# Sparse attention's sliding branch: values and weights in two fp32r parts in place of a native fp32 product, and one ring of rows with one buffer

## The chip, the core and the metric

The program runs on one core of a Trainium2 chip. The metric is the device time of one execution in microseconds (us). A core has TensorE (PE: matrix products; PEld is its loading of stationary operands), VectorE (DVE), ScalarE (ACT), GpSimd (POOL) and SyncE (SP, which here only issues DMAs). Each engine works through its own instructions in a fixed order and waits at an instruction until what it needs has been signalled.

## The reference, cut to what matters

Two blocks of a first kind (stick-breaking and windowed attention, gated, with an MLP) are followed by one block of a second kind: a state-space mixer and a sparse attention, gated and summed, and then a mixture of 32 experts. Sequence 512, width 1024, float32. The change is in the sparse attention. It has 16 heads in two groups of 8, head size 64, and three branches for each head, whose outputs are weighed by gates g:

```
s = q @ k.T * 64 ** -0.5                      # for each branch its own keys
p = softmax(s where the branch's mask allows)
out = g0 * p_cmp @ v_cmp + g1 * p_sel @ v_sel + g2 * p_win @ v_win
```

The compressed branch sees 31 block summaries, the selected branch 4 blocks of 64 tokens, the window branch (window 512, which is the whole sequence, so it is a causal softmax) every earlier token. The change concerns the product `p_win @ v_win` alone.

## The kernel before

Nearly every product is made from operands in two parts: a high part `hi` of type fp32r and the rest `lo = x - hi`, also fp32r, so that `x @ w` is `hi @ w_hi + hi @ w_lo + lo @ w_hi`. `K.split` (line 193 for the subtraction on DVE, line 187 for the high part on POOL) makes the parts. Weights come in 532 tiles of 128x1024: SP loads a raw tile `w_st` (three buffers), POOL writes `w_hi`, DVE writes `w_lo`.

The sparse attention (`Block2.nsa`) walks over 2 groups x 4 token blocks (`tb`), each in 2 halves of four heads, and in each half first the selected branch (`br` 0), then the window branch (`br` 1). `nsa_branch` makes the weights: for each head two products into `ps_b`, a masked minimum on DVE (line 1498, `mx`), an exponential on ACT (line 203, with the sum `sm`), a reciprocal on DVE (line 1500, `ri`) and a scaling on POOL (line 1501), all into a tile `pw`. `nsa_values_sum` then works through the `tb + 1` key blocks: four transposes on TensorE (line 1510) into `ps_tr`, and a copy back to SBUF. For the selected branch the copy is in two parts (`pT`: high part on ACT, line 1517; rest on DVE, line 1518), and two fp32r products with `v2` follow, which holds the high part of the values in columns 0 to 63 and the low part in 64 to 127; both land in `ps_o`, partitions 0 to 63 and 64 to 127. For the window branch one plain float32 copy on ACT (line 1513, tile `pTw`, which shares the slots of `pT` and stands under that name) is followed by one native float32 product with `vw` into the lower 64 partitions of `ps_o`; the hardware runs it as two instruction records. Over all groups, blocks and halves there are 2 x 2 x (1+2+3+4) = 40 such key blocks in each branch. `nsa_put` adds the compressed branch, copies `ps_o`'s upper half (`oh`) and adds both halves.

Dense work is placed between these steps to keep TensorE busy (`fill` in `nsa`): the first state-space projections, whose results go to DRAM through the ring `nf` (`ssm_ahead`, line 997, DMA line 998), and the first group's output projection, also through `nf` (`nsa_out`, line 1647, DMA line 1609). `nf` has two buffers of 128x512. The order of all instructions on each engine is made by a scheduler that plays the program through with a timeline of its own, so that a change in one part can move instructions in later parts.

Of the kernel before, what the change touches and what calls it, by code (L numbers as in the profile page):

```python
# [11 lines left out]
F32R = mybir.dt.float32r  # L12
# [16 lines left out]
# ---------------------------------------------------------------- constants  # L29
# [4 lines left out]
# 1 / theta ** (i / 64) and theta ** (-i / 64), i = 0, 2, .. 62, as float32 gives them  # L34
# [32 lines left out]
class Weights:  # L67
    """Tiles of 1024 columns per partition, taken in one fixed order."""
# [3 lines left out]
    def __init__(self, k, src, total):  # L72
        self.k, self.src, self.total = k, src, total
        self.specs = []
        self.raw, self.ready = {}, {}
        self.loaded = self.made = 0
        self.hold = total       # no tile from here on is cut yet
        self.slots = None       # a part of the program may place tile i itself: slots(i) -> raw, parts (None: not cut)
# [54 lines left out]
class K:  # L133
# [7 lines left out]
    def phase(self, name, alias={}, nbufs={}):  # L141
        """Opens the working pools of a part of the program."""
# [11 lines left out]
    def t(self, shape, tag, dt=F32, bufs=1):  # L154
        """Kept: the slots S0.. and the constants; the rest goes when its phase ends."""
# [11 lines left out]
    def pace(self, every, back=2):  # L167
        """Beats for the products of dense units: each waits for the one `back` before it (0: none).
        They keep the queue of TensorE short, for the steps of a chain between them."""
        self.every, self.back, self.count, self.beats = every, back, 0, []  # L170
# [38 lines left out]
    def rsqrt(self, out, v):  # L209
        """out = v ** -0.5, v [128, n]."""  # L210
        self.nc.gpsimd.tensor_tensor(out, v, self.mhalf.to_broadcast(list(v.shape)), op=OP.pow)

    def rsqrt_act(self, out, v, w, y):
        """The same by ScalarE and VectorE; w and y are scratch of the same shape (y may be out)."""
# [22 lines left out]
    def fm(self, rhs, pieces, evac):  # L237
        """A unit: 128 output features by 512 tokens."""
# [6 lines left out]
    def dense_tm(self, xh, xl, outs, pieces_of, ncols, bank_mates=1):  # L245
        """outs[tb] [128 tokens, ncols] += x[:, tb].T @ w; `bank_mates` outputs share a bank."""
# [38 lines left out]
    def norm_chunk(self, c, x, g, hi, lo):  # L285
        """x [128, 512] of chunk c: g x in two parts, and its squares into the running sum."""
# [16 lines left out]
    def norm_factor(self):  # L303
        """r[token], token major."""
# [12 lines left out]
    def norm_finish(self):  # L317
        """r[token] token major and along the free axis on all partitions."""
# [12 lines left out]
    def o_halves(self, dst, ps_lo, ps_hi, shape):  # L331
        """dst = ps_lo + ps_hi for the two 64-partition halves of a bank."""
# [5 lines left out]
# ---------------------------------------------------------------- first block  # L338
class Block1:
    # dense units between the steps of the stick breaking attention  # L340
    PRE = 6
    PLAN = {3: ("q", 4), 4: ("q", 5), 6: ("g", 6), 7: ("q", 6), 8: ("q", 7), 10: ("g", 7)}
    PACE = (3, 2)       # of the dense units, but for the first
# [88 lines left out]
    def swa_turn(self, tb):  # L432
        """Transposes of q and k of one token block."""
# [75 lines left out]
    def swa(self, r):  # L509
        """Token blocks in a pipeline of four stages, dense units between them."""  # L510
# [154 lines left out]
    def attend(self, xh, xl):  # L665
        """xh, xl [128, 8*512]: parts of g x; the running sum of squares is in k.ssq."""
# [23 lines left out]
    def merge(self, xs, gt, rb):  # L690
# [16 lines left out]
        for m in range(8):  # L707
            g1 = g1s[m // 2][:, m % 2]

            def both(m=m, g1=g1):  # L710
                a, b = k.bank("w2", 2, (P, 2, 512)), None
                # the two branches fill one tile of eight blocks
# [21 lines left out]
    def out_and_mlp(self, ms, x_src, next_norm, between=()):  # L734
        """x_src: DRAM [128, 8, 512]; next_norm(c, x_c) takes each finished chunk of the new x;
        `between` is work for the gaps between the units."""
# [54 lines left out]
G, HG = 4, 8          # state space groups, heads in each  # L791
# [1492 lines left out]
```

## Time and profile before

| what | value |
|---|---|
| time of three runs | 2905.84, 2909.4, 2910.61 us (median 2909.4) |
| span of the profiled execution, first to last instruction | 2902.1 us |
| what lies around the span, against the median | 7.3 us |
| busy share of the span | PE 94%, DVE 65%, POOL 46%, ACT 29% |
| sparse attention's steps between TensorE's dense work | 1660 to 1939 us |
| state space | 1940 to 2300 us |
| experts | 2500 to 2850 us |

The profile is one execution. "Busy" is the union of an engine's instruction times; a matmul's recorded time holds its pipeline latency, so successive records overlap and a fully busy PE can still have idle columns. The distance from one start to the next tells what an instruction costs TensorE. The trace gives for each engine's idle time the instruction that ended it.

### The profile page before, as it was taken

What the parts mean: (1) busy time and instruction counts of PE and PEld (TensorE: products, weight loads), DVE (VectorE), ACT (ScalarE), POOL (GpSimd) and SP (SyncE); (2) the same over time, 40 slices, a digit from 0 to 9 for tenths busy, and PEclk for the clock granted to TensorE, in tenths of its full rate; (3) what the DMA queues carried; (4) which work ended last, traced back from release to release, by engine and by line L of the source; (5) the groups of instructions that cost most, each with busy time, mean ns of one, the idle gap of its engine ahead of it and who ended that gap; (6) DMA issues with size and microseconds to landing.
All of it is one profiled execution on the core that took longest, in us unless ns stands there. A gap on an engine that the chain in (4) does not pass through costs nothing. (4 is left out here: it accounts for less than half of the span.)

```text
span 2902.1 us, 36642 instructions
## 1 busy us (share of the span) xinstructions
PE 2737.3 (94%) x13452; PEld 2211.3 (76%) x13452; DVE 1893.7 (65%) x2911; ACT 840.2 (29%) x1684; POOL 1330.9 (46%) x1718
## 2 busy tenths in 40 slices
PE   7999999999999999999989999999999997888886
PEld 6788788888878877778869887768787876666664
DVE  6865553334486656556545785668677765999898
ACT  3444221021144441201112354462442333211111
POOL 4544244142355423423323454446655652565665
PEclk9999999999999999999999999999999998999988
DMA  4111332223211124556442411222121252677765
GB/s 136 56 61 51 116 95 95 95 99 112 101 59 59 50 96 147 172 176 196 154 154 95 134 56 48 91 85 77 66 80 66 76 211 77 223 270 262 257 236 207
DMA packets 108875, 355.47 MB, mean 122 GB/s; under 512 B 19495, under 2 KB 20391, under 8 KB 108048
## 3 DMA queue, kind: packets, MB, share of 16 engines
q1 hardware_dynamic: 105056, 342.71, 35.3%
q0 software_dynamic: 2592, 6.15, 0.6%
q10 hardware_dynamic: 1040, 4.19, 0.4%
q8 instruction: 108, 1.77, 0.3%
q14 instruction: 79, 0.65, 0.1%
HBM read 329.51 MB, written 27.26 MB: 123 GB/s over the span
## 5 line engine op out<-in xcount | busy, mean ns | idle before, releaser
L165 PE MATMUL ps_d<-S,w_hi 128*128 128x512 f32 x4448 | 1421.0, 397 | 18.6 <-POOL c_eps L181 5.7
L165 PEld LDWEIGHTS ps_d<-S,w_hi 128*128 128x128 f32 x4448 | 827.7, 188 | 204.4 <-POOL c_eps L181 12.2
L165 PE MATMUL ps_d<-S,w_lo 128*128 128x512 f32 x2224 | 877.0, 396 | 14.9 <-DVE w_lo L193 14.6
L187 POOL TENSOR_SCALAR w_hi<-w_st 128x1024 fp32r<-128x1024 f32 x343 | 389.3, 1135 | 743.3 <-PE ps_d L165 610.6
L193 DVE TENSOR_TENSOR w_lo<-w_st,w_hi 128x1024 fp32r<-128x1024 f32 x343 | 453.8, 1323 | 295.4 <-POOL w_hi L187 273.3
L165 PEld LDWEIGHTS ps_d<-S,w_lo 128*128 128x128 f32 x2224 | 418.8, 188 | 112.9 <-DVE w_lo L193 23.2
L203 ACT ACTIVATE f<-ps_d 128x512 f32<-128x512 f32 x64 | 38.4, 600 | 457.3 <-PE ps_d L165 457.3
L181 POOL MEMSET c_eps<- 1x1 f32 x424 | 35.7, 89 | 233.9 <-PE ps_d L165 197.0
L187 POOL TENSOR_SCALAR m_hi<-S 128x1024 fp32r<-128x1024 f32 x81 | 118.4, 1466 | 52.8 <-PE ps_po L165 22.7
L187 POOL TENSOR_SCALAR S<-of 128x512 fp32r<-128x512 f32 x96 | 105.7, 1101 | 67.5 <-DVE of L728 31.3
L193 DVE TENSOR_TENSOR m_lo<-S,m_hi 128x1024 fp32r<-128x1024 f32 x81 | 124.4, 1549 | 13.8 <-POOL m_hi L187 13.8
L862 DVE SCALAR_TENSOR_TENSOR W<-wada,W 128x1024 f32<-128x1024 f32 x48 | 68.5, 1426 | 97.8 <-DMA wada<-in_w_ada_t 97.8
L1501 POOL TENSOR_SCALAR pw<-pw,ri,gn 128x128 f32<-128x128 f32 (+3 forms) x128 | 90.5, 714 | 54.9 <-DVE ri L1500 49.9
L165 PE MATMUL ps_tr<-gS,S 128*128 128x256 f32 x512 | 87.3, 311 | 24.0 <-DVE gS L1917 24.0
L165 PEld LDWEIGHTS ps_tr<-gS,S 128*128 128x128 f32 x512 | 77.9, 208 | 35.8 <-issue 30.4
L193 DVE TENSOR_TENSOR S<-of,S 128x512 fp32r<-128x512 f32 x96 | 79.5, 828 | 33.0 <-POOL S L187 31.0
L165 PE MATMUL ps_w<-w_hi,S 128*128 128x512 f32 x256 | 83.6, 406 | 10.5 <-POOL w_hi L187 10.5
L193 DVE TENSOR_TENSOR w_lo<-S,w_hi 128x1024 fp32r<-128x1024 f32 x53 | 85.9, 1626 | 2.2 <-POOL w_hi L187 2.2
L187 POOL TENSOR_SCALAR w_hi<-S 128x1024 fp32r<-128x1024 f32 x53 | 68.6, 1296 | 26.8 <-PE ps_gu L165 26.8
L165 PE MATMUL ps_w<-S,w_hi 128*128 128x512 f32 x256 | 80.7, 395 | 0.0
L203 ACT ACTIVATE pw<-pw,mx 128x128 f32<-128x128 f32 (+3 forms) x128 | 71.4, 559 | 29.7 <-DVE mx L1498 28.9
L165 PE MATMUL ps_po<-m_hi,mhs 128*128 128x512 f32 x128 | 50.4, 435 | 29.9 <-DVE mhs L193 24.3
(565 smaller groups left out, 4850.2 us busy)
## 6 DMA issues: line engine op xcount, KB each, us to landing
w_st<-in_w SPq DMA_DIRECT2D x374, 512.0 KB, 3.3
S<-in_w SPq DMA_DIRECT2D x158, 512.0 KB, 4.9
wada<-in_w_ada_t SPq DMA_DIRECT2D x48, 512.0 KB, 3.6
x<-S SPq DMA_DIRECT2D x16, 256.0 KB, 2.0
moe_rows<-S ACTq DMA_DIRECT2D x1, 4096.0 KB, 16.5
ssm_away<-nf SPq DMA_DIRECT2D x12, 256.0 KB, 2.0
S<-in_x_t SPq DMA_DIRECT2D x8, 256.0 KB, 6.9
S<-in_x_t SPq DMA_DIRECT2D x1, 2048.0 KB, 8.0
```

Source lines behind the costliest of these rows:

```text
L165: return self.nc.tensor.matmul(out, l, r, start=start, stop=stop, skip_group_check=sk)
L181: b = self.nc.gpsimd.memset(self.beat_at[:, i:i + 1], 0.0)
L187: self.nc.gpsimd.tensor_scalar(hi, x, 1.0, 1.0, op0=OP.mult, op1=OP.mult)
L193: return self.nc.vector.tensor_tensor(lo, x, hi.bitcast(F32), op=OP.subtract)
L203: i = self.nc.scalar.activation(out, x, f, bias=bias, scale=scale, **kw)
L862: nc.vector.scalar_tensor_tensor(junk, w, 1.0, self.cs, op0=OP.mult, op1=OP.mult, accum_out=self.ada[:, j:j + 1])
L1501: nc.gpsimd.tensor_scalar(w, w, ri[:, c], gate[:, c], op0=OP.mult, op1=OP.mult)
```

## The change

The window branch's values get the same treatment as those of the selected branch: `nsa_values` splits both, `v2` has an index for the branch, `vw` goes away. In `nsa_values_sum` both branches take the same path: high part on ACT, rest on DVE, two fp32r products over all 128 columns of `v2`. The ring `nf` has one buffer in place of two.

```diff
 def nsa_values(self, br, src, tb):
-    if br:
-        nc.scalar.copy(self.vw[:, tb], src)
-        return
     vf = k.t([P, 2, 64], "vf", bufs=2)
     nc.scalar.copy(vf, src)
-    k.split(self.v2[:, tb, :, 0:64], self.v2[:, tb, :, 64:128], vf)
+    k.split(self.v2[:, br, tb, :, 0:64], self.v2[:, br, tb, :, 64:128], vf)
...
-    self.v2 = k.t([P, 4, 2, P], "v2", F32R)
-    self.vw = k.t([P, 4, 2, 64], "vw")
+    self.v2 = k.t([P, 2, 4, 2, P], "v2", F32R)
...
 def nsa_values_sum(self, g, tb, br, o, p):
     for j in range(tb + 1):
         pt = k.bank("tr", 2, (P, 4, P))
         for h in range(4):
             nc.tensor.transpose(pt[:, h], p[:, h, j * P:(j + 1) * P], k.ident)
-        if br:
-            w = k.t([P, 4, P], "pTw", bufs=2)
-            nc.scalar.copy(w, pt)
-            k.mm(o[0:64], self.vw[:, j, g], w, False, False, True)
-            continue
         w = k.t([P, 2, 4, P], "pT", F32R, bufs=2)
         nc.scalar.copy(w[:, 0], pt)
         nc.vector.tensor_tensor(w[:, 1], pt, w[:, 0].bitcast(F32), op=OP.subtract)
         for a in range(2):
-            k.mm(o, self.v2[:, j, g], w[:, a], j == 0 and a == 0, False, True)
+            k.mm(o, self.v2[:, br, j, g], w[:, a], not br and j == 0 and a == 0, False, True)
...
-    ... 'pTw': 'pT', ...   {..., 'pT': 2, 'nf': 2, ...}
+    ...                    {..., 'pT': 2, 'nf': 1, ...}
```

Over the program this replaces 40 native products by 80 fp32r products, adds 40 subtractions of 128x512 on DVE, and for the values 4 small splits (POOL and DVE, 128x128). The number of ACT copies stays.

The order on TensorE at the end of the attention, before (group 1, token block 3, second half: the window branch's four key blocks; `ps_tr` are transposes, `vw` the native products):

```order
L165 MATMUL ps_o_16227<-pT_16263,v_1168_11670 128x512
L1510 MATMUL ps_tr_16314<-c_ff_88,pw_16195 128x128 x4
L165 MATMUL ps_o_16227<-pT_16311,vw_11671 64x512
L1510 MATMUL ps_tr_16322<-c_ff_88,pw_16195 128x128 x4
L165 MATMUL ps_o_16227<-pT_16319,vw_11671 64x512
L1510 MATMUL ps_tr_16330<-c_ff_88,pw_16195 128x128 x4
L165 MATMUL ps_o_16227<-pT_16327,vw_11671 64x512
L165 MATMUL ps_o_16227<-pT_16335,vw_11671 64x512
L165 MATMUL ps_o_16227<-cT_15836,vcd_12901 128x128 x8
```

And at the same place in the changed kernel (both branches now read `v`, which is `v2`):

```order
L165 MATMUL ps_o_16310<-pT_16346,v_1168_11670 128x512
L1506 MATMUL ps_tr_16399<-c_ff_88,pw_16278 128x128 x4
L165 MATMUL ps_o_16310<-pT_16394,v_1168_11670 128x512
L1506 MATMUL ps_tr_16409<-c_ff_88,pw_16278 128x128 x4
L165 MATMUL ps_o_16310<-pT_16404,v_1168_11670 128x512 x2
L165 MATMUL ps_o_16310<-pT_16414,v_1168_11670 128x512
L1506 MATMUL ps_tr_16419<-c_ff_88,pw_16278 128x128 x4
L165 MATMUL ps_o_16310<-pT_16414,v_1168_11670 128x512
L165 MATMUL ps_o_16310<-pT_16424,v_1168_11670 128x512 x2
L165 MATMUL ps_o_16310<-cT_15905,vcd_12912 128x128 x8
```

Each native product has become a product with the high part and one with the rest. The last dense product (`ps_d`) ahead of the attention's end stands earlier against the steps than before: 15 native window products and 14 selected key blocks came after it, now 32 key blocks of both kinds.

DVE at the same place, before (the last rows of the attention; `S<-ps_o,oh` is `nsa_put`):

```order
L1535 TENSOR_TENSOR S_1300_12916<-ps_o_16040,oh_16191 64x2x128 x2
L1518 TENSOR_TENSOR pT_16243<-ps_tr_16238,pT_16243 128x512
L1500 RECIPROCAL ri_16198<-sm_16197 128x1
L193 TENSOR_TENSOR S_1924_16385<-S_1300_12916,S_1923_16384 128x512 x2
L1518 TENSOR_TENSOR pT_16253<-ps_tr_16248,pT_16253 128x512
L1518 TENSOR_TENSOR pT_16263<-ps_tr_16258,pT_16263 128x512
L1535 TENSOR_TENSOR S_1300_12916<-ps_o_16227,oh_16346 64x2x128 x2
```

And in the changed kernel:

```order
L1526 TENSOR_TENSOR S_1303_12927<-ps_o_16115,oh_16274 64x2x128 x2
L1509 TENSOR_TENSOR pT_16326<-ps_tr_16321,pT_16326 128x512
L1509 TENSOR_TENSOR pT_16336<-ps_tr_16331,pT_16336 128x512
L193 TENSOR_TENSOR S_1927_16476<-S_1303_12927,S_1926_16475 128x512 x2
L1509 TENSOR_TENSOR pT_16346<-ps_tr_16341,pT_16346 128x512
L1509 TENSOR_TENSOR pT_16394<-ps_tr_16389,pT_16394 128x512
L1509 TENSOR_TENSOR pT_16404<-ps_tr_16399,pT_16404 128x512
L1509 TENSOR_TENSOR pT_16414<-ps_tr_16409,pT_16414 128x512
L1509 TENSOR_TENSOR pT_16424<-ps_tr_16419,pT_16424 128x512
L1526 TENSOR_TENSOR S_1303_12927<-ps_o_16310,oh_16437 64x2x128 x2
```

Four subtractions of the window branch now stand between the last scores and the attention's last sum.

Far behind, in the experts, the scheduler moves rows too. POOL, after a page of expert rows is written to DRAM (`moe_rows`, an indirect DMA; `mhs` is the high part of an expert's hidden values, `m_hi` and `w_hi` those of weight tiles), in the kernel before:

```order
L2016 DMA moe_rows<-my_21612,idx_20743 1024x1024
L187 TENSOR_SCALAR mhs_2404_20546<-mhe_21662 128x64
L187 TENSOR_SCALAR m_hi_21711<-S_2420_20659 128x1024
L187 TENSOR_SCALAR w_hi_21860<-S_2464_20804 128x1024
L187 TENSOR_SCALAR m_hi_21851<-S_2420_20659 128x1024
```

And in the changed kernel behind one such page:

```order
L2007 DMA moe_rows<-my_21472,idx_20834 1024x1024
L187 TENSOR_SCALAR w_hi_21720<-S_2477_20931 128x1024
L187 TENSOR_SCALAR w_hi_21767<-S_2495_20996 128x1024
L187 TENSOR_SCALAR mhs_2405_20635<-mhe_21619 128x64
L187 TENSOR_SCALAR m_hi_21711<-S_2477_20931 128x1024
```

Before, `mhs` stood right behind `moe_rows` at 9 places; now at none, at least one weight tile's high part stands between them.

## Rows read from the trace of the kernel before

**Rows 1.** The page's head and the busy time of each engine.

```profile
span 2902.1 us, 36642 instructions
PE 2737.3 (94%) x13452; PEld 2211.3 (76%) x13452; DVE 1893.7 (65%) x2911; ACT 840.2 (29%) x1684; POOL 1330.9 (46%) x1718
```

**Rows 2.** Busy time of each engine in four stretches.

```profile
core 0: us, PE busy (x) PEld busy (x) DVE busy (x) ACT busy (x) POOL busy (x), PEclk, DMA share, GB/s
1660.00:1879.00 219.00, 218.46 (x1274) 172.11 (x1273) 152.35 (x521) 110.12 (x301) 106.53 (x243) 1.00 0.19 66
1879.00:1939.00 60.00, 55.58 (x281) 34.34 (x281) 38.22 (x122) 37.94 (x88) 26.59 (x35) 1.00 0.15 50
1940.00:2300.00 360.00, 352.32 (x1766) 286.54 (x1765) 266.94 (x345) 130.89 (x248) 218.43 (x196) 1.00 0.23 79
2500.00:2850.00 350.00, 299.24 (x1419) 229.06 (x1419) 311.60 (x301) 62.55 (x172) 217.99 (x183) 0.94 0.76 256
```

**Rows 3.** Tile `pT`, 1660 to 1940: duration in ns min/median/max, first and last start.

```profile
L165 PE MATMUL ps_o<-pT,vw x80: 592/593/644, 1676.5 to 1937.6; 128*64 128x512 f32 x80
L1517 ACT CAST pT<-ps_tr x40: 572/587/594, 1665.5 to 1929.9; 128x512 fp32r<-128x512 f32 x40
L1518 DVE TENSOR_TENSOR pT<-ps_tr,pT x40: 673/686/693, 1668.4 to 1931.1; 128x512 fp32r<-128x512 f32 x40
L1513 ACT COPY pT<-ps_tr x40: 564/586/592, 1672.8 to 1936.4; 128x512 f32<-128x512 f32 x40
```

**Rows 4.** Timeline of TensorE at the attention's end: start us, length us.

```profile
1928.25 1.17 PE L165 MATMUL ps_o<-pT,v 128*128 128x512 f32 x4 [1.21 <-ACT pw L203]
1929.25 0.60 PE L1510 MATMUL ps_tr<-c_ff,pw 128*128 128x128 f32 x4
1929.68 0.50 PE L165 MATMUL ps_o<-pT,v 128*128 128x512 f32 x1
...
1931.20 0.73 PE L165 MATMUL ps_o<-pT,v 128*128 128x512 f32 x2 [1.02 <-DVE pT L1518]
...
1936.21 1.93 PE L165 MATMUL ps_o<-pT,vw 128*64 128x512 f32 x4
1938.08 1.11 PE L165 MATMUL ps_o<-cT,vcd 128*128 128x128 f32 x8
...
1939.54 0.63 PE L165 MATMUL ps_d<-S,w_hi 128*128 128x512 f32 x2
1940.01 0.40 PE L165 MATMUL ps_d<-S,w_lo 128*128 128x512 f32 x1
```

**Rows 5.** Groups of VectorE, 1879 to 1939: busy us, mean ns, idle before.

```profile
L1498 DVE CUSTOM_DVE_ANT_0 pw<-ps_b,S 128x512 f32<-128x512 f32 (+1 forms) x12 | 7.2, 639 | 0.4 <-POOL S L1481 0.4
L1500 DVE RECIPROCAL ri<-sm 128x1 f32<-128x1 f32 x26 | 3.8, 157 | 4.2 <-ACT pw L203 4.1
```

**Rows 6.** Tile `nf` (DVE, DMA), then SP's timeline, 1843 to 1880.

```profile
L1647 DVE TENSOR_TENSOR nf<-ps_d,S x8: 677/692/693, 1843.6 to 1878.2; 128x512 f32<-128x512 f32 x8
DMA to landing us min/median/max: 2.0/2.0/3.9
...
1866.06 2.90 SPq L1609 DMA_DIRECT2D y_nsa<-nf  x2
```

**Rows 7.** Timelines of POOL, then DVE, in the experts.

```profile
2592.72 1.03 POOL L2016 DMA_INDIRECT moe_rows<-my,idx  x1 [3.68 <-DVE mhd L1949]
2609.38 3.99 POOL L187 TENSOR_SCALAR m_hi<-S 128x1024 fp32r<-128x1024 f32 x2
...
2594.08 4.07 DVE L193 TENSOR_TENSOR mhs<-mhe,mhs 128x64 fp32r<-128x64 f32 x1 [1.38 <-POOL mhs L187]
2608.43 4.03 DVE L193 TENSOR_TENSOR w_lo<-S,w_hi 128x1024 fp32r<-128x1024 f32 x2
```

**Rows 8.** Lone durations beside those: DVE `w_lo`, POOL `m_hi`, 2590 to 2625.

```profile
2602.32 1.21 DVE L193 TENSOR_TENSOR w_lo<-S,w_hi 128x1024 fp32r<-128x1024 f32 x1
2596.03 1.03 POOL L187 TENSOR_SCALAR m_hi<-S 128x1024 fp32r<-128x1024 f32 x1
```

More of the change, by code (lines that the diff above doesn't have):

```diff
@@ L2237, in program @@
     b2.yn = [dram.tile([P, KC, T], F32, name=f"y_nsa{i}") for i in range(2)]
-    ph = k.phase("n", {'s1': 'b', 'hidv': 'q2T', 'hids': 'cT', 'hid': 'cs', 'kr': 'qr', 'vf': 'pT', 'vc': 'pT', 'pTw': 'pT',
+    ph = k.phase("n", {'s1': 'b', 'hidv': 'q2T', 'hids': 'cT', 'hid': 'cs', 'kr': 'qr', 'vf': 'pT', 'vc': 'pT',
                        'yf': 'pT', 'hp': 'pT', 'k2': 'cT'},
-                 {'b': 3, 'o': 1, 'q2T': 2, 'cT': 2, 'cs': 2, 'qr': 1, 'pT': 2, 'nf': 2, 'igt': 1, 'ieq': 1})
+                 {'b': 3, 'o': 1, 'q2T': 2, 'cT': 2, 'cs': 2, 'qr': 1, 'pT': 2, 'nf': 1, 'igt': 1, 'ieq': 1})
     b2.Y = dram.tile([2 * T, D], F32, name="moe_rows")
```

## Prediction

> **What bounds the kernel now.** I read the page's head first [rows 1]: PE is busy for 94% of a span of 2902.1 us, and no other engine for more than 65%. That is an average, so the next view is busy time by stretches [rows 2]. From 1660 to 1879 us, the part of the sparse attention that has dense products between its steps, PE is busy for 218.5 of 219 us at a granted clock of 1.00, DVE for 152.4 (70%). From 1879 to 1939 the dense products are used up: PE is busy for 55.6 of 60 us, DVE for 38.2, ACT for 37.9, so PE still leads, but it begins to wait for the chain. From 1940 to 2300 PE leads again (352.3 of 360). In the experts, 2500 to 2850, DVE leads with 311.6 of 350. The change touches the first two stretches, and the scheduler rearranges the other two.
>
> Next comes what one key block costs PE, from start to start. Four records of the native product begin at 1936.21 and the next kind at 1938.08: 1.87 / 4 = 0.47 us a record, two records a product, 0.94 us. Four fp32r records take 1.00 us (1928.25 to 1929.25), 0.25 each; two in dense work 0.47 (1939.54 to 1940.01), 0.235 each [rows 4].
>
> **The change part by part.**
>
> *PE.* 40 products at 0.94 go, 80 fp32r records at 0.235 to 0.25 come: a product falls to 0.47 to 0.50, so 0.44 to 0.47 is saved each time, about 0.45. In sum 40 x 0.45 = 18.0 us of TensorE's time.
>
> *ACT.* Its copy stays: 586 ns at line 1513 against 587 at line 1517 [rows 3]. Nothing.
>
> *DVE.* 40 more subtractions at 0.686 us [rows 3], 27.4 us. The existing 40 lie between 673 and 693 ns, whatever POOL did, so I take no stretching. The eight small splits of the values (DVE, POOL) come near 1590 us, under dense products, and cost nothing; without that cover they would be under 3 us by half a subtraction each.
>
> *Where the DVE time lies.* In the order of the changed kernel the last dense product stands earlier against the steps, so the stretch without cover grows. Counted there from the last dense evacuation on: DVE has 32 subtractions (14 before), 32 minima (26), 33 reciprocals (27) and one more set of short selection steps. Priced: 18 x 0.686 = 12.3; 6 minima at about 0.6 [rows 5] (639 ns for the mix) 3.6; 6 x 0.157 = 0.9; the selection steps about 2. DVE's work in this stretch goes from 38.2 to 57.0 us. PE there: 15 native products out (-14.0), 36 fp32r records in (+9.0), 18 transposes at 0.11 (four in 0.43, from 1929.25 to 1929.68 [rows 4], +2.0) and 10 score products at about 0.18 (three quarters of 0.235, +1.8): 55.6 - 1.2 = 54.4. DVE becomes the longest by a little. Before, the leader was busy for 55.6 of 60, 93%; with two engines almost level in one chain I take 90%: 57.0 / 0.9 = 63 us, 3 more than now. The bounds are 57 (DVE never waits) and 71 (80%).
>
> *The first stretch.* PE gives up 18.0 - 1.2 = 16.8 of 218.5: 201.7, with today's half microsecond of idle 202. DVE there has 152.4 + 27.4 - 18.8 = 161.0 us, 80% in place of 70%. PE's instructions wait more often for a rest on DVE: I allow 2 us (bounds 0 and 7), as the rare waits of this kind in the trace are about 1 us (1931.20 waits 1.02 for `pT` [rows 4]). 204 in place of 219.
>
> *Attention in sum:* 204 + 63 = 267 against 279: 12 us less. Bounds 202 + 57 = 259 (20 less) and 209 + 71 = 280 (1 more).
>
> *Ring `nf`.* A writer now waits until the DMA before it has landed, 2.0 us after its issue (3.9 at most), and its own write takes 0.69 [rows 6]. The closest pair of issues stands at 1866.06, two issues within 2.90 us less the 0.33 of one: 2.57 us apart. Needed are 2.0 + 0.69 + about 0.1 = 2.8. So one wait of 0.2 us on DVE, under dense products: nothing. Bounds 0 and 5 us, if the writes crowd together now that PE is faster; a waiting evacuation holds the later minima on DVE's queue, and PE then waits for scores.
>
> *Moved rows.* In the state space PE leads at 98%, and an order costs or gives little there: 0, bounds +-3. In the experts `mhs` no longer stands right behind `moe_rows`. Today POOL waits at `moe_rows` for 3.68 us, DVE then waits 1.38 for `mhs`, and its 64-column operation lasts 4.07, while POOL runs four weight tiles [rows 7]. At 9 places that is 9 x 1.38 = 12.4 us of DVE's idle time. What comes back depends on what DVE and POOL can do side by side. Alone, a rest takes 1.21 and a high part 1.03 us [rows 8], 2.24 together; interleaved, two of each take about 4.0 (the pairs at 2608.43 and 2609.38 [rows 7]), 2.0 together. So the two hardly overlap, and idle time of one is mostly work of the other. I take 1 us less, with bounds of 12 less (all of the waits come back) and 10 more (the new order opens nearly as many). The Trainium skill, "SBUF — State Buffer", section "Who interferes with whom", says that a DVE instruction with two SBUF inputs and a GpSimd instruction that reads SBUF exclude each other for the whole instruction. By that rule the sum for a pair would be 2.24, not 2.0, and less would come back; the rows decide for 2.0.
>
> **Sum.** 12 + 1 = 13 us less. The profiled execution's span of 2902.1 would become 2889. The median of the three runs is 2909.4, 7.3 above that span; I carry the difference over: 2909.4 - 13 = **2896 us**. Within 0.2% (5.8 us) is about what a measurement of this kernel can't tell from no change.
>
> **The rivals.**
>
> *DVE eats the gain.* The uncovered stretch is then not 63 but 71 us, and the first gives up only 10 in place of 15, since PE waits for rests: 209 + 71 = 280, or less badly 206 + 68 = 274, which is 0 to 5 us gained, 2904 to 2910. For it: DVE, ACT and PE form one chain there, and PE's 18 us can only be used where something else is ready. Against it: DVE would still be idle for a fifth of the stretch. The point that decides: DVE's busy share in the stretch, 80% or 90%. A rule of the Trainium skill speaks for this one: "Trainium Kernel Development and Optimization", section "Best Practices", holds that the busy share of matmuls tells little of how near the limit TensorE is, and that the share of weight loading is the better sign. That share is 172.1 of 219 in the first stretch, 79%, and 34.3 of 60 in the second, 57% [rows 2]; by it PE wouldn't limit the second stretch even now, and little of the 18 us would show. The starts in rows 4 say otherwise for the dense part.
>
> *All of it shows.* DVE keeps up everywhere (259 us for the attention), or the experts return their waits: 20 or more less, 2883 to 2890. For it: DVE at 80% in the first stretch. Against it: ACT and POOL stand in the same chain.
>
> *Slower by the ring.* 20 writes go through `nf`; if each waited for the landing of the one before (2.0 us) and PE for the writer, that would be 19 x 2.0 = 38 us, less 12: 26 slower, 2935. It decides against the change from 0.9 us of wait a write on (0.9 x 19 + 1 = 18). Against it: the gaps of 2.57 us and more. The experts' order could add its 10 to a small gain and end near 2916; it is the likelier half of this case.
>
> **How the numbers follow.** My forecast (2890 to 2904, likeliest 2896) 0.48; all of it shows 0.17; DVE eats the gain 0.23; slower 0.12. The range leaves out the far part of the slower case and the tip of the fast one: 2883 to 2910. Faster by over 0.2% (below 2903.6): 0.17 and nearly all of 0.48, 0.64. Slower (above 2915.2): 0.11. The same: 0.25.
>
> **What the profile would show.** Right: no native record in `ps_o`; 160 fp32r records there; 80 subtractions at 0.69; PE still at 99% up to the last dense product, which comes some 15 us or more earlier; then a stretch of about 63 us with DVE at 90%. Wrong, if PE waits for `pT` of DVE in many places of the first stretch, if writers of `nf` wait for a DMA for more than 1 us each, or if the experts' stretch differs by more than 6 us either way.

## The result and the profile after

The changed kernel takes 2920.6 us (median of five runs, 2918.9 to 2930.4) against 2906.7 before (five runs, 2902.9 to 2910.6): 1.0051 times as long, interval 1.0039 to 1.0064. It is 14 us slower, where 13 us faster was forecast. The profiled execution is the slowest of its five, so I read lengths of stages from it and take the whole from the medians.

The page's head after, beside [rows 1]:

```profile
span 2928.5 us, 36686 instructions
PE 2741.1 (94%) x13452; PEld 2239.3 (76%) x13452; DVE 1893.1 (65%) x2955; ACT 842.8 (29%) x1685; POOL 1342.1 (46%) x1722
```

The shares are those of before, to the percent. Nothing is to be seen at this height, and the stages have to be laid side by side. I cut them at instructions that both kernels have. "First stretch": from the first transpose of weights (`ps_tr` from `pw`) to the start of the last write into `nf`, that is while there are dense products. "Rest": from there to the end of the last sum of heads (`S` from `ps_o`). "Routing": from the last product into `ps_b` to the first into `ps_po`. "Experts": from there to the start of the last product into `ps_po`. The busy time of each engine in these four, changed kernel (columns as in [rows 2]):

```profile
1670.76:1878.81 208.05, 199.81 (x1215) 174.07 (x1213) 155.69 (x497) 101.75 (x276) 96.45 (x227) 0.97 0.19 65
1878.81:1950.32 71.51, 58.43 (x320) 43.67 (x320) 55.62 (x171) 45.31 (x106) 30.01 (x42) 0.98 0.13 43
2449.83:2517.83 68.00, 47.44 (x246) 41.85 (x247) 61.49 (x121) 25.11 (x52) 32.38 (x28) 0.69 0.44 147
2517.83:2905.98 388.15, 328.78 (x1476) 250.28 (x1475) 314.36 (x308) 63.81 (x171) 250.35 (x194) 0.92 0.72 246
```

and in the kernel before:

```profile
1664.82:1878.18 213.36, 212.82 (x1243) 167.44 (x1242) 147.78 (x500) 107.03 (x290) 102.22 (x233) 1.00 0.19 64
1878.18:1940.68 62.50, 58.08 (x293) 36.27 (x292) 39.87 (x126) 39.92 (x92) 28.40 (x36) 1.00 0.15 49
2438.04:2503.11 65.07, 43.08 (x238) 38.09 (x239) 60.39 (x120) 24.09 (x49) 31.30 (x28) 0.76 0.43 146
2503.11:2879.47 376.36, 319.75 (x1483) 241.87 (x1482) 336.19 (x311) 64.05 (x173) 242.40 (x194) 0.94 0.75 254
```

The attention (first two rows) went from 275.9 to 279.6 us, +3.7 in place of -12. Experts went from 376.4 to 388.1, +11.8 in place of -1, and routing from 65.1 to 68.0, +2.9, which I had not priced. The rest of the spans' 26.4 us is +4.4 up to the first product into `ps_b` (1511.05 to 1515.42 us), where both kernels have the same instructions and other executions scatter as much, +1.6 from there to the first stretch, and +2.1 in the state space.

In the first stretch PE is idle for 8.2 us (208.05 - 199.81; 0.5 before) and the clock is 0.97. In the rest it is idle for 13.1 (4.4 before), at 0.98. So 21.3 us of waiting stand against 5.0, and a mean clock of 0.97 means that some 6% of 208 us, 12 to 14 us, ran at half clock (1.2 GHz). What TensorE waited for, in the attention of the changed kernel (total, times, longest, us):

```profile
PE ps_o L165 <- DVE pT L1509: 5.8, 13, 1.5
PE ps_d L165 <- DVE qt L1256: 3.1, 1, 3.1
PE ps_tr L1449 <- POOL cs L1446: 3.0, 1, 3.0
PE ps_tr L1420 <- DVE S L1410: 2.0, 1, 2.0
```

Only 5.8 us are waits for a subtraction (`pT`, of either branch), and only 0.7 of them, two waits, lie in the first stretch. The longest single waits are for other steps: `qt` rotates the next group's queries and so frees the bank `ps_d`, `S` (line 1410) is the low part of these queries that TensorE turns next, and `cs` are the weights of the next compressed branch. VectorE while TensorE waited for `qt` (idle from 1747.8 to 1750.8), then TensorE after the wait, as timelines:

```profile
1745.17 0.68 DVE L1509 TENSOR_TENSOR pT<-ps_tr,pT 128x512 fp32r<-128x512 f32 x1
...
1748.59 0.84 DVE L1526 TENSOR_TENSOR S<-ps_o,oh 64x256 f32<-64x256 f32 x2
1749.46 0.59 DVE L1460 TENSOR_REDUCE pcs<-cs 128x32 f32<-128x256 f32 x1
1749.96 0.41 DVE L1254 TENSOR_TENSOR qr<-ps_d,c_rope 128x256 f32<-128x256 f32 x1
1750.29 0.48 DVE L1256 TENSOR_TENSOR qt<-ps_d,c_rope 128x128 f32<-128x128 f32 x2
```

```profile
1750.83 0.38 PE L165 MATMUL ps_d<-w_hi,S 128*128 128x256 f32 x1 [3.06 <-DVE qt L1256]
...
1752.30 1.06 PE L1506 MATMUL ps_tr<-c_ff,pw 128*128 128x128 f32 x4
```

VectorE works through its queue without a gap of note (10.62 of the 11 us from 1739 to 1750), and the rotation that TensorE needs stands at the end of it. Just behind the wait, four transposes take 1.06 us in place of 0.60. The stretch at half clock in three windows, before, in and after it:

```profile
1747.50:1751.50 4.00, 0.94 (x7) 0.67 (x6) 3.62 (x13) 0.50 (x1) 3.61 (x8) 1.00 0.01 2
1751.60:1755.00 3.40, 3.40 (x18) 3.40 (x17) 2.48 (x9) 0.96 (x2) 0.53 (x4) 0.50 0.00 0
1755.10:1759.00 3.90, 3.90 (x32) 3.73 (x32) 1.44 (x4) 1.19 (x3) 1.40 (x6) 1.00 0.00 0
```

PE was busy for 0.94 of 4 us, then ran 3.4 us at 1.2 GHz, the lower of its two levels (18 records where the next 3.9 us have 32), though it had work. The same follows the wait for `S` at 1781.94 and the one for `cs` at 1907.5. But the longest stretch at half clock, some 6.8 us from 1703.9 on, stands behind no long wait. Ahead of it are three short ones, 1.3 us together (timeline of TensorE, then the row of these 20 us):

```profile
1700.83 0.47 PE L165 MATMUL ps_o<-pT,v 128*128 128x512 f32 x1 [0.24 <-ACT pT L1508]
1701.91 0.50 PE L165 MATMUL ps_b<-S,q2T 128*128 128x256 f32 x2 [0.62 <-DVE mx L1494]
1702.86 0.74 PE L165 MATMUL ps_o<-pT,v 128*128 128x512 f32 x2 [0.45 <-DVE pT L1509]
```

```profile
1700.00:1720.00 20.00, 18.69 (x121) 17.46 (x120) 14.44 (x56) 10.22 (x30) 7.30 (x23) 0.83 0.09 34
```

In the kernel before the attention has no such stretch (clock 1.00 in both rows).

### The profile page after: what moved, and what is told of

It is laid out like the page before. It is cut to its first block, busy times and chain, and to the rows that moved or that the text cites. A ratio compares the mean times of both kernels' runs of the same rounds, so it can differ in the third digit from the quotient of the medians.

```text
span 2928.5 us, 36686 instructions
## 1 busy us (share of the span) xinstructions
PE 2741.1 (94%) x13452; PEld 2239.3 (76%) x13452; DVE 1893.1 (65%) x2955; ACT 842.8 (29%) x1685; POOL 1342.1 (46%) x1722
## 4 chain that ended last, share of the span: by engine, by line
PE 70%; DVE 12%; POOL 6%; issue 5%; DMA 4%; ACT 2%; DVEq 0%; POOLq 0%; SPq 0%; ACTq 0%
PE ps_d L165 44%; PE ps_w L165 8%; PE ps_b L165 3%; PE ps_o L165 3%; DMA wada<-in_w_ada_t 3%; DVE w_lo L193 3%; PE ps_po L165 2%; PE ps_e L165 2%; PE ps_gu L165 2%; PE ps_tr L165 2%; POOL w_hi L187 1%; DVE m_lo L193 1%; PE ps_s L165 1%; POOL m_hi L187 1%; DVE pw L1494 1%
## 5 line engine op out<-in xcount | busy, mean ns | idle before, releaser
L1497 POOL TENSOR_SCALAR pw<-pw,ri,gn 128x128 f32<-128x128 f32 (+3 forms) x128 | 87.1, 689 | 61.7 <-DVE ri L1496 55.0
L165 PEld LDWEIGHTS ps_tr<-gS,S 128*128 128x128 f32 x512 | 84.0, 226 | 37.1 <-issue 15.9
L1917 ACT CAST S<-ps_tr 128x256 fp32r<-128x256 f32 x128 | 43.9, 375 | 129.8 <-PE ps_tr L165 116.5
```

Of the source, the lines that this page charges most:

```text
L165: return self.nc.tensor.matmul(out, l, r, start=start, stop=stop, skip_group_check=sk)
L1497: nc.gpsimd.tensor_scalar(w, w, ri[:, c], gate[:, c], op0=OP.mult, op1=OP.mult)
L1917: nc.scalar.copy(x[:, :, c], ps[:, :, i * P:(i + 1) * P].rearrange("p a (e s) -> p e a s", s=SLOTS))
```

## The experiments

Instructions named as in the change; lengths by the same cuts, from the one profiled execution of each kernel, ratios from the timed runs beside the kernel before.

| run | first + rest = attention | routing | experts | experts' order | ratio to before |
|---|---|---|---|---|---|
| before | 213.4 + 62.5 = 275.9 | 65.1 | 376.4 | before | 1 |
| changed | 208.0 + 71.5 = 279.6 | 68.0 | 388.1 | changed | 1.0051 (1.0039 to 1.0064) |
| e1_sub_only | 208.9 + 72.0 = 280.9 | 67.8 | 388.0 | changed | 1.0056 (1.0039 to 1.0073) |
| e2_no_sub | 203.8 + 61.7 = 265.4 | 65.5 | 382.1 | before | 0.9998 (0.9985 to 1.0010) |
| e3_nf_only | 217.4 + 61.3 = 278.7 | 67.2 | 382.7 | a third | 1.0038 (1.0024 to 1.0052) |
| e4_before_fill | 237.9 + 48.9 = 286.8 | 66.2 | 374.5 | before | 1.0042 (1.0026 to 1.0059) |
| f1_after_order_before | 205.2 + 71.5 = 276.7 | 65.5 | 377.2 | before, held | 1.0023 (1.0013 to 1.0033) |
| f2_before_order_after | 213.3 + 62.5 = 275.8 | 68.1 | 384.7 | changed, held | 1.0045 (1.0031 to 1.0058) |
| f3_hybrid | 211.8 + 69.5 = 281.3 | 65.1 | 381.8 | before, held | 1.0008 (0.9999 to 1.0017) |
| f4_priority | 200.8 + 66.9 = 267.7 | 65.8 | 379.2 | before, held | 0.9971 (0.9960 to 0.9982) |
| g1_before_priority | 214.2 + 61.7 = 275.8 | 65.3 | 377.1 | before, held | 0.9997 (0.9985 to 1.0008) |
| g2_ring | 217.5 + 61.3 = 278.7 | 65.1 | 381.8 | before, held | 1.0013 (1.0004 to 1.0022) |
| g3_priority_free | 200.8 + 66.6 = 267.4 | 67.2 | 383.6 | nearly changed | 0.9994 (0.9984 to 1.0004) |
| g4_hybrid_priority | 206.9 + 66.5 = 273.4 | 65.0 | 381.9 | before, held | 0.9976 (0.9965 to 0.9987) |

### VectorE's work without TensorE's saving, and the reverse

`e1_sub_only`, on the kernel before:

```diff
-                w = k.t([P, 4, P], "pTw", bufs=2)
-                nc.scalar.copy(w, pt)
-                k.mm(o[0:64], self.vw[:, j, g], w, False, False, True)
+                w = k.t([P, 2, 4, P], "pT", bufs=2)
+                nc.scalar.copy(w[:, 0], pt)
+                nc.vector.tensor_tensor(w[:, 1], pt, w[:, 0], op=OP.subtract)
+                k.mm(o[0:64], self.vw[:, j, g], w[:, 0], False, False, True)
```

> The kernel before, with 40 more subtractions of 128x512 on VectorE whose results nobody reads (the native product stays, its copy takes the low half of a buffer of the changed kernel's size). Attention (first transposes of weights to the last sum of the heads) is 275.9 us in the kernel before and 279.6 in the changed one. Theory 'VectorE's time': 27 us more of VectorE's queue ahead of minima and rests make TensorE wait, with no saving against it: 282 to 292. Rival 'the dependency': only because the second product waits for its subtraction does TensorE wait; with nobody waiting, 275 to 278. The experts' rows stand here in the order of the changed kernel. Theory 'the order': from the first to the last product of the experts 384 to 392 us, as in the changed kernel (388.1), not 376.4 as before; if the order is not the cause, 373 to 380.

Attention 280.9, +5.1: just under the span of the first theory, well over that of the rival. The subtractions cost time although nobody reads them, but less than I expected of them; TensorE has no wait for one of them, its waits for the old steps grew. No stretch ran at half clock:

```profile
1666.13:1875.02 208.89, 207.51 (x1207) 163.39 (x1206) 157.85 (x504) 100.69 (x274) 98.80 (x228) 1.00 0.18 65
1875.02:1947.05 72.03, 64.57 (x329) 41.52 (x328) 54.53 (x162) 45.47 (x107) 30.80 (x41) 1.00 0.13 43
```

The experts took 388.0 us, to 0.2 us what they take in the changed kernel, though this kernel has the native product and both buffers. It stands in the changed kernel's order.

`e2_no_sub`, on the changed kernel:

```diff
-            nc.vector.tensor_tensor(w[:, 1], pt, w[:, 0].bitcast(F32), op=OP.subtract)
+            if not br:
+                nc.vector.tensor_tensor(w[:, 1], pt, w[:, 0].bitcast(F32), op=OP.subtract)
             for a in range(2):
-                k.mm(o, self.v2[:, br, j, g], w[:, a], ...
+                k.mm(o, self.v2[:, br, j, g], w[:, 0 if br else a], ...
```

> The changed kernel, whose window branch leaves out the subtraction: its second product takes the high part a second time, so the low part of the weights is left out of the result there. TensorE's work is that of the changed kernel, VectorE's that of the kernel before. Theory 'VectorE's time': the 18 us of TensorE's saving come out nearly whole, attention 258 to 265 us, and no dip of the granted clock in it. Rival 'latency': the stretch behind the last dense product is a chain whose length hardly hangs on VectorE's load, so it stays at about 70 us and the attention at 270 to 276. The experts' rows stand here in the order of the kernel before: theory 'the order' gives 372 to 380 us for them; if the order is not the cause, 384 or more.

Attention 265.4, -10.5, 0.4 over the first theory's span; the rest fell to 61.7, so it does hang on VectorE's load, against the rival. Two things missed: the clock did dip (0.99 and 0.97), and of TensorE's 18 us only 10.5 came out, since PE now sat idle for 14.1 us (203.76 - 198.91 and 61.65 - 52.40):

```profile
1670.47:1874.23 203.76, 198.91 (x1234) 172.43 (x1233) 147.65 (x488) 104.21 (x282) 99.78 (x230) 0.99 0.19 67
1874.23:1935.88 61.65, 52.40 (x303) 41.66 (x302) 42.29 (x138) 42.35 (x101) 29.03 (x39) 0.97 0.15 50
```

A faster TensorE alone thus runs into waits. Experts 382.1, between the two spans. The whole equals before all the same: 10.5 us came in the attention, and in the profiled execution 5.8 went in the experts and 5.6 ahead of the attention, 1.6 of them for the small splits. The medians of ten and fifteen runs agree too, so chance in one execution hardly explains it; what takes the gain back in this kernel isn't settled.

### The ring

`e3_nf_only`, on the kernel before: `'nf': 2` becomes `'nf': 1`.

> The kernel before with one buffer in the ring of rows, and nothing else. Theory 'VectorE's time': the ring costs nothing, attention 275 to 278 us. Rival 'the ring': it takes a good part of the 15 us that the forecast was wrong by, 280 us or more, with VectorE waiting for a DMA in several places. The experts stand in a third order, so this shows a third value for them: between 372 and 392 us by the theory 'the order', 376 by its rival.

Attention 278.7, between the two theories. To see the ring without the experts' third order, `g2_ring` is the same edit with the experts held in the order of before (how, under the next heading).

> The kernel before with one buffer in the ring of rows, experts held in the order of the kernel before. In the run with the ring alone the attention took 278.7 us, 2.8 more, and the experts, in a third order, 382.7. Theory 'the order': here the experts fall to 374 to 382 and what is left is the ring, 0 to 3 us, the whole 2905 to 2911. Rival 'the ring': 2913 or more, as with the ring alone (2915).

Attention 278.7 again, the same to 0.1 us. The whole is 2914.1, which by the number is the rival's; but the kernel before took 2908.6 beside it, and 2904.9 beside the ring alone. So it is 5.5 us by the medians and 3.8 by the ratio of 1.0013, where the ring alone had 10.2 and 11.0. The ring costs about 2.9 us in the attention, the upper end of what I expected, and the third order a good part of the rest. VectorE's waits for the landing of the buffer before, in the two runs and in the changed kernel:

```profile
DVE nf L1647 <- DMA y_nsa<-nf: 4.7, 2, 2.8
DVE nf L1655 <- DMA y_nsa<-nf: 2.9, 1, 2.9
DVE nf L1638 <- DMA y_nsa<-nf: 5.2, 2, 3.8
```

PE is idle for 6.3 us in place of 5.0 (217.45 - 215.43 and 61.26 - 56.98 in the second run). Where the other 1.5 us go isn't settled.

### The experts' order

`e4_before_fill`, on the kernel before: `AHEAD = {0: range(10), 3: range(8, 10)}` becomes `{0: range(10), 3: range(6, 10)}`.

> The kernel before with two more dense units of the state space (24 products each, 5.6 us) taken ahead into the attention. Attention longer by the 11 us of these units less the 4 to 5 us of idle time that they can fill: 281 to 287 us; the state space shorter by about 11 us; in sum 0 to 5 us gained up to the experts. The experts stand in the order of the changed kernel: theory 'the order' 384 to 392 us, and the whole 4 to 10 us slower than before; if the order is not the cause 373 to 380, and the whole faster.

The premise was wrong: its experts stand in the order of the kernel before (`mhs` right behind `moe_rows` at 9 places), and they take 374.5 us, as the theory then has it. The attention grew by 10.9 as said, but the state space shrank by only 0.4 us, since PE was idle there for 20.0 us in place of 12.3. So dense work taken ahead gained nothing here.

To hold an order, `f1_after_order_before` and `f2_before_order_after` give each instruction from the routing to the last expert an edge to the one that precedes it on its engine in the other kernel's order. Such an edge fixes the place in the queue and adds no wait.

```diff
+    def pin(self):
+        base = int(self.mark.ins.name[2:])
+        by = {i.name: i for i in k.nc.cur_bb.bb.instructions}
+        for engine, steps in PINS.items():
+            names = [f"I-{base + n}" for n in np.cumsum([int(x) for x in steps.split()])]
+            for x, y in zip(names, names[1:]):
+                k.tc.add_manual_dep(by[y], x, NOSYNC, reason="order")
```

> The changed kernel, whose instructions of the experts and the routing ahead of them are held on every engine in the order of the kernel before; the attention is the changed one. Theory 'the order': the experts (first to last product) fall from 388.1 to between 374 and 382 us and the routing by about 2.5, so the whole is 9 to 15 us faster than the changed kernel, 2906 to 2912, within 0.2% of the kernel before; the attention stays at 277 to 282. Rival 'what the attention leaves behind' (weights loaded later, another phase of the clock): the experts stay above 384 and the whole above 2915.

> The kernel before, whose experts and routing are held in the order of the changed kernel; native products, two buffers in the ring. Theory 'the order': experts 385 to 391 us and routing about 68, the whole 9 to 15 us slower than the kernel before, 2914 to 2920, although nothing of the change is in it. Rival 'what the attention leaves behind': experts 373 to 380, the whole within 4 us of the kernel before.

The first came out, but for the attention, 0.3 below its span, and the ratio, a little over 0.2%: the changed kernel with the old order has 377.2 and 65.5 us, and takes 2911.7 us in place of 2920.6, 8.9 less. So did the second, but for the experts' 384.7, 0.3 below the span: the old kernel with the new order takes 2917.9 against 2907.2 beside it, 10.7 more, with nothing of the change in it. The rival is out both ways.

The attention of the first, 276.7 us, is that of the changed kernel in order and in waits (the ten longest are the same to 0.1 us). It lacks the long stretch at half clock; the same 20 us of work here, with the same three short waits (0.24, 0.61 and 0.45):

```profile
1695.60:1715.60 20.00, 18.63 (x143) 17.22 (x142) 16.95 (x59) 11.13 (x31) 9.04 (x26) 1.00 0.09 33
```

TensorE gets through 143 records in place of 121, and the first stretch takes 205.2 us in place of 208.0. So nearly all of the 2.9 us between 279.6 and 276.7 is that stretch at half clock, which the same order and the same waits brought in one execution and not in the other.

What the new order does is read from the waits, of the changed kernel first, then of the same kernel with the old order. VectorE for high parts:

```profile
DVE m_lo L193 <- POOL m_hi L187: 38.8, 28, 3.2
DVE w_lo L193 <- POOL w_hi L187: 22.2, 14, 2.7
DVE mhs L193 <- POOL mhs L187: 1.6, 7, 0.2
```

```profile
DVE m_lo L201 <- POOL m_hi L195: 18.4, 14, 2.3
DVE mhs L201 <- POOL mhs L195: 13.8, 17, 1.4
DVE w_lo L201 <- POOL w_hi L195: 3.9, 3, 1.7
```

and POOL for the hidden values, in the same two:

```profile
POOL mhs L187 <- DVE mhe L1938: 39.9, 14, 5.9
```

```profile
POOL mhs L195 <- DVE mhe L1955: 25.2, 9, 3.6
```

The waits at `mhs` that I hoped to get back did come back (13.8 to 1.6 us). But POOL now stands longer at `mhs`, with weight tiles queued behind it, and VectorE waits for those tiles: 61.0 us in place of 22.3. VectorE's own operations at `mhs` also got shorter, in the same two:

```profile
L193 DVE TENSOR_TENSOR mhs<-mhe,mhs 128x64 fp32r<-128x64 f32 x31 | 17.3, 558 | 2.2 <-POOL mhs L187 1.6 <-ACT mhs L190 0.2
```

```profile
L201 DVE TENSOR_TENSOR mhs<-mhe,mhs 128x64 fp32r<-128x64 f32 x32 | 47.0, 1470 | 14.1 <-POOL mhs L195 13.8
```

So the new order gave back 29.7 us of VectorE's busy time there and 12 of its waits, more than the forecast's best bound, and the experts still became longer, while its waits for the weight tiles grew by 38.7. That the longer stand at `mhs` is what starves VectorE is my reading of these rows; the runs show only that the order does it.

With one order the experts still vary from kernel to kernel (one profiled execution each, so chance isn't told from the kernel's own): over nine profiled executions in the order of before 374.5 to 382.1 (mean 379.1), over three in the changed order 384.7 to 388.1 (386.9). The longer ones have the lower clock: 0.92 in the rows of e2_no_sub and g2_ring (382.1, 381.8), 0.94 before and in e4_before_fill (376.4, 374.5). What sets it isn't settled.

### Where the subtractions cost

`f3_hybrid`, on the changed kernel: parts for group 0 only, and for group 1 `vw`, a plain copy and the native product, as before the change.

```diff
+            if br and g:
+                w = k.t([P, 4, P], "pTw", bufs=2)
+                nc.scalar.copy(w, pt)
+                k.mm(o[0:64], self.vw[:, j], w, False, False, True)
+                continue
```

> Window branch in two parts in group 0 alone, which lies under dense products throughout; group 1, whose end has none, with native products; one buffer in the ring; experts in the order of the kernel before. TensorE saves 20 x 0.45 = 9 us, VectorE has 20 more subtractions. Theory 'VectorE's time' (it costs most where no dense product covers it): the stretch behind the last dense product is near that of the kernel before (62 us for like content), the attention 269 to 274 us, the whole 1 to 7 us faster than before. Rival 'the waits of the steps': with DVE's queue longer in group 0 too, TensorE waits there and the clock dips, attention 275 or more, no gain.

The rival came out: attention 281.3, no gain, clock 0.97 in the first stretch, and TensorE waits for the same steps as in the changed kernel, 3.1 us for `qt` and 2.0 for `S`. So the uncovered end is not the only place where the subtractions cost. Group 0, which I had taken to be covered by dense products, is one too.

`f4_priority`, on the changed kernel, experts held in the order of before:

```diff
                     if i < 7 and br == 1 and half == 0:
-                        nq = turn(i + 1)
+                        with k.tc.high_priority():
+                            nq = turn(i + 1)
                     if i < 7 and br == 0 and half == 1:
-                        nsb, ncT = self.nsa_compressed(*steps[i + 1], nq)
+                        with k.tc.high_priority():
+                            nsb, ncT = self.nsa_compressed(*steps[i + 1], nq)
```

> The changed kernel, with the turning of the next block's queries and the next compressed branch put ahead in the scheduler's order, experts in the order of the kernel before. In the changed kernel TensorE's longest waits in the attention are for these steps (3.06 us for the rotated queries, 1.99 for the turned ones, 3.05 and 0.85 for the compressed branch), and each is followed by a stretch at half clock. Theory 'the steps stand behind the subtractions on VectorE': these waits go, with the dips behind them, attention 266 to 274 us, the whole 3 to 10 us faster than before. Rival: VectorE's work is only moved, and the last key blocks wait instead, 277 to 282.

As the theory said: attention 267.7, the whole 2897.3 against 2907.2 (0.9971), 14 us less than the same without priority (f1_after_order_before, 2911.7). Of these 9.0 are in the attention; in the profiled executions the state space is 5.4 shorter too (493.9 for 499.3), which I hadn't forecast and haven't followed up. Priority moves more than VectorE's steps: the turning for group 1 begins with the products of its queries. The wait for `qt` fell from 3.1 to 0.6 us, the one for `S` is gone, and so are the stretches at half clock in the first stretch; the wait for `cs` stays, with some 6.8 us at half clock from 1890.4 on:

```profile
1666.05:1866.88 200.83, 196.95 (x1232) 171.21 (x1230) 158.64 (x513) 104.47 (x281) 98.73 (x230) 1.00 0.20 68
1866.88:1933.73 66.85, 56.83 (x303) 42.75 (x303) 51.16 (x154) 42.83 (x101) 28.86 (x40) 0.95 0.14 46
```

```profile
PE ps_tr L1457 <- POOL cs L1454: 2.5, 1, 2.5
PE ps_d L173 <- DVE qt L1264: 0.6, 1, 0.6
```

Is that priority's gain or the change's? `g1_before_priority` makes the same edit on the kernel before.

> The kernel before with the same two steps put ahead as in the run 'priority' (turning of the next queries, next compressed branch), native products, two buffers in the ring, experts in the order they have in the kernel before. Theory 'the steps stood behind the subtractions': without the subtractions TensorE hardly waited (5.0 us in 275.9), so there is nothing to gain, attention 272 to 277, the whole within 4 us of the kernel before; the 10 us gained by the changed kernel with priority are then the change's own gain, set free. Rival 'priority alone': the kernel before gains the same 7 to 10 us, attention 265 to 270, and the change is worth nothing even so.

Attention 275.8, the whole 0.9997 (0.9985 to 1.0008): priority alone is worth nothing there. The gain belongs to the change, and priority sets it free. The last two runs ask what is needed beside it. `g3_priority_free` holds no order, `g4_hybrid_priority` splits group 0 alone:

> The changed kernel with the two steps put ahead, and nothing held: the scheduler orders the experts itself, nearly as in the changed kernel. Attention 265 to 270 us as with the held order (267.7); theory 'the order': experts 384 to 392, the whole 8 to 12 us slower than with the held order, 2905 to 2910, so the same as the kernel before. Rival: experts below 382, the whole below 2902.

> Two parts in group 0 alone, native products in group 1, and the two steps put ahead; experts in the order of the kernel before. The split alone gave 277 to 280 us for the attention, priority took 9 to 12 off. Theory 'the steps stood behind the subtractions': priority takes the waits for the rotated and the turned queries (3.1 and 2.0 us, with three dips) out here as well, attention 267 to 273, the whole 2897 to 2903; it is not faster than two parts everywhere with priority, unless the stretch behind the last dense product gains more from 16 subtractions fewer than TensorE loses by its native products (66.8 us there against 69.5 in the hybrid).

Without the held order the attention is the same (267.4), the experts take 383.6, 0.4 below the theory's span, and the whole is 0.9994, no different from before: 10.4 us lost to the order by the medians, some 7 by the two ratios. The hybrid with priority comes to 273.4, 0.4 over the theory's span, and 0.9976; at 2903.0 it is not faster than two parts everywhere (2897.3). The kernel f4_priority beats the kernel before by 0.3% and the changed one by 0.8%.

## Why the prediction was wrong, point by point

**TensorE's saving** was right. With the waits mostly gone, in f4_priority, PE is busy for 253.8 us in the attention (196.95 + 56.83) against 270.9 before, 17.1 less for 18.0 forecast, with some 7 us of it at half clock (a mean of 0.95 over 66.9 us).

**DVE's work** was right in sum: 55.6 us in the rest for 57.0 forecast, 155.7 in the first stretch for 161.0, in a window 5.6 us longer, which held 4.6 us more of it before.

**The step that failed first** is "with two engines almost level in one chain I take 90%", and with it the 63 us for the rest, 3 more than before. VectorE is busy for 55.62 of 71.51 us, 78%, and the rest grew by 9.0 (from 62.50). That is the point named in the rival "DVE eats the gain" (80%, 11 more). Beside it stands "I allow 2 us" for waits in the first stretch: they were 8.2 us, over even the bound of 7, and some 13.6 us ran at half clock. The first stretch gave up 5.3 us, where I had 15 and the rival 10. In sum the rival had 1 us more for the attention; it took 3.7 more, and 0.8 more in f1_after_order_before. Both steps, as I read it, failed for one reason: I reckoned VectorE's load as an average, 70% rising to 80%, and looked at subtractions that TensorE itself waits for. Of the three signs of being wrong that I named, the ring and the experts came; many waits for `pT` in the first stretch did not. The load comes in bursts. The trace of before had it, in windows of 20 us:

```profile
1720.00:1740.00 20.00, 19.82 (x122) 14.70 (x122) 19.15 (x73) 12.77 (x35) 12.65 (x23) 1.00 0.09 28
1760.00:1780.00 20.00, 19.64 (x110) 14.02 (x109) 17.22 (x55) 10.56 (x25) 8.29 (x20) 1.00 0.08 27
```

At 96% there was hardly room for a subtraction of 0.686 us every few us, and what stood last in that queue in the changed kernel was a step that TensorE needs next. Putting these steps ahead took the waits for `qt` and `S` out (f4_priority), and was worth nothing without the subtractions (g1_before_priority). The price of the 27 us hangs on TensorE's slack: 5.1 us of attention with native products (e1_sub_only), 11 to 14 with the faster ones (279.6 or 276.7 against 265.4).

**The clock** was no term of the sum, and should have been: each of the changed kernel's waits of 2 to 3 us in the attention was followed by 3.4 us at half clock, and three short waits once by 6.8. The Trainium skill, "TensorE: Matmul & The Clock Gate", section "HAM oscillation — how this bites in real kernels", describes waits between groups of products that make the next group start at the lower clock. The rows at 1751.60 agree, though here the first 0.8 us after the wait (from 1750.83) still ran at the higher clock.

**The small splits** "cost nothing", I said, "under dense products". TensorE waits for them, 1.5 and 0.8 us between 1575 and 1605 us in the changed kernel, where it waited once for 0.7 before:

```profile
PE ps_tr L1280 <- POOL cT L187: 1.5, 1, 1.5
PE ps_b L165 <- DVE w_lo L193: 0.8, 1, 0.8
```

The +1.6 us ahead of the first stretch are these; all executions with both groups split have 155.2 to 155.4 us there, all others 153.0 to 153.8.

**The ring**, "one wait of 0.2 us", was two waits of 5.2 us together, and 2.9 us of the attention when it is changed alone. The gaps between writes that I took from before were not the fault: in the changed kernel writes begin 2.8 us apart without a wait (1857.22, 1860.03, 1862.87), as priced. The length of a wait was. In the longest one of each of the three kernels the next write begins 3.1 to 3.7 us after the issue of the one before, where I had 2.1 (2.0 to landing and 0.1), and each time SP issued a load of weights 0.8 to 1.1 us ahead of it; here g2_ring, SP and then VectorE:

```profile
1850.67 0.33 SPq L85 DMA_DIRECT2D w_st<-in_w  x1
1851.76 4.27 SPq L1617 DMA_DIRECT2D y_nsa<-nf  x2
...
1854.98 0.69 DVE L1655 TENSOR_TENSOR nf<-ps_d,S 128x512 f32<-128x512 f32 x1 [2.92 <-DMA y_nsa<-nf]
```

That the load holds the write up isn't tested. The cost lies within the bounds of 0 and 5.

**The experts** are the larger half. I took 1 us less, with bounds of 12 less and 10 more; the order costs 8.9 to 10.7 us, routing included. The step that failed is "idle time of one is mostly work of the other", which looked at the wait that would go, and not at the one that the new order opens: VectorE's waits for weight tiles, 38.7 us more. The case "slower" named this (the experts' 10 against a small gain, near 2916), as the likelier half of its 0.12. I had no row that could tell the sign, and the forecast should have carried both signs with equal chance.

In sum, the 14 us by the medians are some 9 to 11 for the order and some 4.5 by the medians, 6.7 by the ratio (f1_after_order_before, 1.0023), for the change itself: 18 us saved on TensorE, and more than given back in waits behind VectorE's queue, at half clock, in the ring and in the small splits. These parts are read from single executions and do not add up to the whole to better than some 5 us.

## What to carry to other kernels

Before adding work to an engine that is "only 70% busy", read its busy time in short windows (20 us here), and ask which later step stands behind the new instruction in that queue; putting that step ahead may be worth more than the change. Here a saving on the leading engine turned into waits, and into a lower clock, since the engines behind it couldn't follow. Where a scheduler makes the order, a change moves instructions far away, and that can outweigh it: hold the order to tell the two apart.

## What the runs showed of the hardware

After a single wait of 2 to 3 us in otherwise dense work TensorE ran 3.4 us at 1.2 GHz while it had work, as in the row at 1751.60, and four transposes took 1.06 us in place of 0.60. In f4_priority it was 6.8 us, after a wait of 2.54. The length of a wait doesn't tell it alone. In the kernel before, a wait of 2.07 us in the state space (up to 2235.68) was followed by no lower clock, and one of 1.71 us (up to 2383.84) by some 3.4 us of it. Three waits of 0.24, 0.62 and 0.45 us were followed by 6.8 us at 1.2 GHz in the changed kernel, and the same three by none in f1_after_order_before.
